# One inference step of a hybrid decoder layer in float32: two tiles of a sum trade places, and two cache copies move to another stage

## The chip, the cores and the metric

The kernel runs on one core of a Trainium2 chip. The metric is the device time of one execution in microseconds. The engines are named as in the profile: PE is the matrix engine, PEld its weight loads, DVE the vector engine, ACT the scalar engine, POOL the GpSimd engine, SP the engine that here only issues DMAs. Each engine works through its own list of instructions in order; DMAs issued by SP or ACT run on hardware queues (q1 and q10 in the profile), those issued by POOL on a software queue (q0). All of them share the sixteen DMA engines.

## What is computed

One decoder layer and a final norm for two groups of requests with the same weights: a prompt of 1024 positions and 8 samples of 8 positions, together 1088 columns. Everything is float32.

```python
def hybrid_layer(x, k_past, v_past, conv_b_past, conv_f_past, ...):
    xn = rmsnorm(x, norm1_g)
    q, k, v, glu_a, glu_b, gate_a, gate_b = jnp.split(xn @ w_in, SPLIT_IDX, axis=-1)
    ...
    branch_a = attn @ w_o_attn                    # sliding window attention, 128 wide
    u = glu_a * jax.nn.sigmoid(glu_b)
    c = dwconv_valid(jnp.concatenate([conv_b_past, u], axis=1), conv_b_w, conv_b_bias)
    branch_b = jax.nn.silu(layernorm(c, ln_b_g, ln_b_b)) @ w_pb
    merged = jax.nn.sigmoid(gate_a) * branch_a + jax.nn.sigmoid(gate_b) * branch_b
    h = x + merged @ w_out
    up = rmsnorm(h, norm2_g) @ w_up
    uc = dwconv_valid(jnp.concatenate([conv_f_past, up], axis=1), ffn_conv_w, ffn_conv_b)
    gate, val = jnp.split(uc, 2, axis=-1)
    y = h + (jax.nn.silu(gate) * val) @ w_down
```

The model width is 1024, the inner width of the feed-forward part 2816 (22 blocks of 128). Among the outputs are the new windows of the key and value caches of the samples, `concatenate([k_past, k])[:, -128:]`. Of each window 120 rows are old ones, taken over unchanged. The kernel copies them from the inputs `kpT` and `vp` to the outputs `o_kwp` and `o_vwp`, in DRAM, 960 KB each. No tile is involved.

## The kernel before

**Arithmetic.** A float32 product is made of three matmuls on rounded halves (`mm3`, L190 to L194): high times high (L192), high weight times low operand (L193), low weight times high operand (L194). Whatever goes into a matmul is therefore split first: `split_ps` (L226 to L228) makes the high half with a cast on ACT (L227) and the low half with a subtraction on DVE (L228). Weights are loaded in float32 into `wraw` (L150, L254 for the first ones) and split in the same way (L173, L174 or L227, L228).

**Stages, in the order of the program.** First the norm and the input projection, in chunks of 384, 384 and 320 columns. `norm1_load` (from L237) brings x in parts of one or two of its eight blocks of rows on SP (L242) between parts of the first three weights (L254), some of which ACT and POOL issue. `norm1_raw` splits x (L278, L279) for the first chunk, whose weights' products are scaled only afterwards; the later chunks are normed first (L347 to L349), with factors that small matmuls with an identity matrix (`identr`, cast on POOL at L847) spread over the partitions (L336). Attention, the convolution of branch B and its layer norm follow. Then comes branch A's projection (`do_o`): its result is multiplied by a gate (tile `ga`, L1010, DVE) into one of two buffers `ma`, and stored to DRAM by POOL (L1011).

`phase_z` is the projection of branch B. It computes the product of four halves with fewer multiplications, so it needs sums of the operand's quarters, T1 to T4. Each sum has two parts j, each with a high half (y = 0) and a low half (y = 1). The tiles of T1 to T3 are called `t` + x + j + y, where x counts from 0: `t111` is the low half of T2's second part, `t211` the low half of T3's second part. They are twelve tiles of 128 x 4 x 272 values in one pool, `tb`, opened when branch A's buffers are given back, and laid one behind the other in the order of `T_PLACES` (L45, L1064). A tile of the pool may be written only when whatever lay in the same bytes before is read for the last time. For the buffers `ma` that is when their store has landed.

The output projection with the second norm follows, then the feed-forward part. `ffn_up` makes the gate and value products, two blocks f = 0 and 1 plainly and the others in pairs, in the same manner with sums of quarters. Each block starts with `up_start` (L1375): a tile `st` whose first two columns are cleared on POOL (L1378), and in which the old rows of the samples are put by another POOL instruction (L1383). At f = 5 the two copies of the caches stand between these two, issued by POOL (L1381, L1382) and bound to the memset with `issue_after`. `finish` does the convolution over three positions (L1401 on ACT, L1403 on DVE), the gating and the stores (L1418 and L1424, POOL).

`ffn_down` is the last stage: two plain blocks of the down projection, `product(0)`, another plain block, `product(1)`, and the last block with the final norm. `product` calls functions from a table `hooks` at given steps (m, p) of its loop; at (0, 0) of `product(1)` two calls of `residual` (L1668) add h from DRAM to the accumulator H with an accumulating DMA on POOL.

**What sets the order.** The program only names the instructions; a planner orders each engine's list when the program is made. It takes instructions by priority, which is the place in the program plus an offset given with `self.later`, among those that are ready in its own planned time: whose inputs are made and whose buffers are free. `tc.issue_after(x)` binds an instruction behind x on its engine. On the chip each engine then keeps this order.

Of the kernel before, what the change touches and what calls it, by code (L numbers as in the profile page):

```python
# [17 lines left out]
NT = 8  # L18
# [23 lines left out]
AHEAD = 3  # L42
UP_LATER = 100
GATE_AFTER = 30
T_PLACES = ("000", "001", "200", "201", "210", "100", "211", "111", "010", "011", "101", "110")  # L45
SPLIT_AFTER = 4
GATE_LATER = 60
DOWN = ((0, 1), (2, 3), (16, 17), (18, 19, 20, 21))
# [74 lines left out]
class Build:  # L123
# [898 lines left out]
    def phase_z(self, s_es, sp, xw, sb):  # L1022
# [40 lines left out]
        at = {}  # L1063
        for tag in T_PLACES:  # L1064
            at[tag] = self.t(tb, [P, KT // 2, QW], "t" + tag, F32R)
# [267 lines left out]
    def ffn_up(self, hh, hl, mp):  # L1333
        nc, tc, a, pool = self.nc, self.tc, self.a, self.pool
# [40 lines left out]
        def up_start(f):  # L1375
            st = self.t(ft, [P, FW], "st", bufs=4)
            ss = st[:, 2 + SEQ:].rearrange("p (b t) -> p b t", b=NB)
            z = nc.gpsimd.memset(st[:, 0:2], 0.0)  # L1378
            if f == 5:
                with tc.issue_after(z.ins):  # L1380
                    nc.gpsimd.dma_start(a["o_kwp"], a["kpT"][:, :, :, NT:])  # L1381
                    nc.gpsimd.dma_start(a["o_vwp"], a["vp"][:, NT:, :])  # L1382
            nc.gpsimd.tensor_copy(ss[:, :, 0:2], co[:, f, 2:].rearrange("p (b t) -> p b t", b=NB))  # L1383

            def parts(c):
                o, n = QUARTERS[c]
                m = min(n, SEQ - o)
                yield st[:, 2 + o:2 + o + m], lambda v: v[:, :m]
                if m < n:
                    yield ss[:, :, 2:], lambda v: v[:, m:n].rearrange("p (b t) -> p b t", b=NB)  # L1390

            def ev(c, o, n, ps):
                for d, r in parts(c):
                    nc.scalar.copy(d, r(ps))
            return st, ss, parts, ev
# [40 lines left out]
        def plain(f):  # L1436
            fs = (f, NF + f)
            ws = [self.weight(("up", x), 2 - n if f == 0 else 1) for n, x in enumerate(fs)] if f == 0 else [None] * 2
            both = [up_start(x) for x in fs]
            if f == 0:  # L1440
                for c in range(4):
                    for w, b in zip(ws, both):
                        self.stream(None, xs, b[3], chunks=(c,), w=w, table=QUARTERS)
            else:
                for x, b in zip(fs, both):
                    self.stream(("up", x), xs, b[3], chunks=range(4), table=QUARTERS)
            if f == 0:
                with self.later(-60):
                    sums()
            finish(f, both, PLAIN_LATER)  # L1450
# [75 lines left out]
        def pair(f):  # L1526
            base = 7 * (f - PLAIN)
            (_, _, pg, _), (_, _, pv, _) = both = [up_start(x) for x in (f, NF + f)]
            banks = {}
            copy = nc.scalar.copy  # L1530
# [82 lines left out]
    def ffn_down(self, mp):  # L1613
        nc, a = self.nc, self.a
# [19 lines left out]
        def a_prep(n):  # L1634
            add = nc.vector.tensor_tensor
            while len(tiles) < min(n, 56):
                p = len(tiles) % 7
                a11, a21, a12, a22 = raws[len(tiles) // 7]
                r = {0: a11, 5: a12, 6: a22}.get(p)
                if r is None:  # L1640
                    sums[p] = r = self.t(aw, [P, 3, P], "as", bufs=3)
                    x, y, op = ((a21, a22, ALU.add), (a11, sums.get(1), ALU.subtract), (a12, sums.get(2), ALU.add),
                                (a21, a11, ALU.subtract))[p - 1]
                    add(r, x, y, op)
                t = self.t(aw, [P, 3, 2, P], "aw", F32R, bufs=A_AHEAD + 2)
                self.split_ps(t[:, :, 0, :], t[:, :, 1, :], r)
                tiles.append(t)
                a_load()
# [16 lines left out]
        gated = lambda f: self.g_split(f, self.g_load(f, row()), mp)  # L1665
# [7 lines left out]
        def product(s, hooks):  # L1673
            for m in range(4):
                banks = {}
                for p, (bank, fresh, row, c) in enumerate(seq):
                    n = 28 * s + 7 * m + p
                    a_prep(n + 1 + A_AHEAD)
                    w = tiles[n]
                    for j in range(2):  # L1680
                        if fresh:
                            banks[bank, j] = self.bank("mm" if bank == "A" else "aux")
                        ps = banks[bank, j][:, :QW]
                        cs = slice(j * QW, (j + 1) * QW)
                        for x in range(3):
                            b = ops[s, p, x]
                            self.mm3(ps, w[:, x, 0], w[:, x, 1], b[:, 0, cs], b[:, 1, cs], fresh and x == 0, x == 2,
                                     not fresh)
                        hs = H[:, row + m, (c + j) * QW:(c + j + 1) * QW]
                        self.added = nc.vector.tensor_tensor(hs, hs, ps, ALU.add).ins  # L1690
                    for go in hooks.get((m, p), ()):
                        go()

        def each(f, xs):
            return [lambda x=x: f(x) for x in xs]
# [25 lines left out]
        for m in range(3):  # L1721
# [2 lines left out]
        late = {divmod(2 * x, KT): [lambda i=x + 10: second(i)] for x in range(11)}  # L1724
        late[2, 2] = [lambda: a_prep(28 + A_AHEAD + 2)] + late[2, 2]
        self.down(2, H, None, late)
        product(1, {(0, 0): each(residual, (3, 7)), (2, 0): [unit], (2, 2): [unit], (2, 4): each(gated, (18,)),
                    (2, 6): each(gated, (19,)), (3, 0): each(gated, (20,)), (3, 1): [unit] + each(gated, (21,)),
                    (3, 2): [unit]})
        a_es.close()  # L1730
# [191 lines left out]
```

## Time and profile before

| | |
|---|---|
| runs | 1653.41, 1653.29, 1651.78 us; median 1653.29 |
| profiled execution | 1655.33 us, span 1653.5 us, mean granted PE clock 0.998 |
| PE, PEld | busy 1641.8 us and 1625.1 us, 11,606 matmuls |
| DVE | 1372.9 us, 2,474 instructions |
| ACT | 865.5 us, 1,795 instructions |
| POOL | 260.3 us, 551 instructions |
| DMA | 200.48 MB, 121 GB/s over the span |
| q1 (SP) | 128.52 MB, 25.0% of sixteen engines |
| q0 (POOL) | 69.75 MB, 14.2% |

The page cuts the span into forty slices of 41.3 us. This is the busy share of some of them in tenths (9 is 90% or more), and what the DMA engines did:

```profile
PE   9999999999999999999999999999999999999998
DVE  7899979999979996787755887698888787989867
POOL 0100112221011111121003421142222110000000
PEclk9999999999999999999999999999999999999999
DMA  6221222223121255647763533243333334766403
```

How to read it: PE is busy in every slice, so its gaps are too short to show here and have to be looked for in its waits and in the timeline. A timeline row is start, duration, engine, line, operation, tile written and tiles read, the shape, how many equal instructions are drawn together (x2), and in brackets the idle time of the engine just before it with the instruction that the profile takes for its releaser. A row of stretches has the stretch, its length, the busy time and count of instructions of PE, PEld, DVE, ACT and POOL, then PE's granted clock (1 is full speed), the busy share of the DMA engines and GB/s. A DMA row has the size and the time from issue to landing.

### The profile page before, as it was taken

The numbers are of one execution on the slowest core, as the hardware profiler recorded it, in microseconds if no ns is written. First come the engines' busy times: TensorE is split into PE (matmuls) and PEld (weight loads), VectorE is DVE, ScalarE is ACT, GpSimd is POOL, SyncE is SP. The second block draws the span as 40 slices with busy tenths as digits, with TensorE's granted clock in tenths as the row PEclk, the third lists the DMA queues.
The fourth block names the chain that finished last, engine by engine and source line by source line (L and its number), as shares of the span: only waits on it lengthen the run. The fifth ranks groups of instructions, "written<-read, shape, count | busy, mean of one in ns | idle before, by whom it ended". The sixth has DMA issues, their size and how long they took to land. (4 is left out here: it accounts for less than half of the span.)

```text
span 1653.5 us, 30189 instructions
## 1 busy us (share of the span) xinstructions
PE 1641.8 (99%) x11606; PEld 1625.1 (98%) x11606; DVE 1372.9 (83%) x2474; ACT 865.5 (52%) x1795; POOL 260.3 (16%) x551
## 2 busy tenths in 40 slices
PE   9999999999999999999999999999999999999998
PEld 9999999999999999999999999999999999999997
DVE  7899979999979996787755887698888787989867
ACT  6524378774488845585533454454444454524222
POOL 0100112221011111121003421142222110000000
PEclk9999999999999999999999999999999999999999
DMA  6221222223121255647763533243333334766403
GB/s 209 84 66 47 65 71 75 94 98 96 51 61 45 86 204 178 199 162 195 194 223 105 186 110 127 77 137 114 116 109 115 98 100 135 259 162 164 109 14 109
DMA packets 102497, 200.48 MB, mean 121 GB/s; under 512 B 23904, under 2 KB 54640, under 8 KB 102336
## 3 DMA queue, kind: packets, MB, share of 16 engines
q1 hardware_dynamic: 78864, 128.52, 25.0%
q0 software_dynamic: 23056, 69.75, 14.2%
q8 instruction: 91, 1.49, 0.4%
q14 instruction: 54, 0.44, 0.1%
q10 hardware_dynamic: 432, 0.27, 0.1%
HBM read 136.44 MB, written 64.03 MB: 121 GB/s over the span
## 5 line engine op out<-in xcount | busy, mean ns | idle before, releaser
L192 PE MATMUL mm<-xh,whi 128*128 128x384 f32 (+1 forms) x904 | 301.3, 333 | 0.0
L193 PE MATMUL mm<-xl,whi 128*128 128x384 f32 (+1 forms) x904 | 295.4, 327 | 0.2
L194 PE MATMUL mm<-xh,wlo 128*128 128x384 f32 (+1 forms) x904 | 295.5, 327 | 0.0
L193 PEld LDWEIGHTS mm<-xl,whi 128*128 128x128 f32 x904 | 170.0, 188 | 1.6 <-DVE xl L279 0.8
L192 PEld LDWEIGHTS mm<-xh,whi 128*128 128x128 f32 x904 | 169.9, 188 | 0.7
L194 PEld LDWEIGHTS mm<-xh,wlo 128*128 128x128 f32 x904 | 169.7, 188 | 0.1
L1403 DVE SCALAR_TENSOR_TENSOR acc<-st,fc,acc 128x1104 f32<-128x1104 f32 x88 | 119.9, 1364 | 3.7 <-ACT acc L1401 2.4
L173 ACT CAST whi<-wraw 128x1024 fp32r<-128x1024 f32 (+1 forms) x65 | 62.7, 970 | 72.9 <-PE mm L193 52.7
L227 ACT CAST whi<-wraw 128x512 fp32r<-128x512 f32 x84 | 52.6, 626 | 77.0 <-PE aux L194 36.9
L227 ACT CAST wlo<-wraw 128x512 fp32r<-128x512 f32 x84 | 52.6, 626 | 73.5 <-PE aux L194 41.3
L522 DVE SCALAR_TENSOR_TENSOR bt<-u,consts,bt 128x513 f32<-128x513 f32 x120 | 89.7, 747 | 0.7
L522 DVE SCALAR_TENSOR_TENSOR c<-sm,hsum,c 128x512 f32<-128x512 f32 x120 | 89.5, 746 | 0.7
L192 PE MATMUL mm<-mh,whi 128*128 128x272 f32 (+4 forms) x296 | 88.2, 298 | 0.0
L194 PE MATMUL mm<-mh,wlo 128*128 128x272 f32 (+4 forms) x296 | 87.9, 297 | 0.0
L228 DVE TENSOR_TENSOR wlo<-wraw,wlo 128x512 fp32r<-128x512 f32 x84 | 60.7, 723 | 29.0 <-ACT wlo L227 27.8
L522 DVE SCALAR_TENSOR_TENSOR c<-u,consts,c 128x512 f32<-128x512 f32 x112 | 83.5, 746 | 0.6
L193 PE MATMUL mm<-ml,whi 128*128 128x272 f32 (+4 forms) x280 | 82.9, 296 | 0.0
L228 DVE TENSOR_TENSOR whi<-wraw,whi 128x512 fp32r<-128x512 f32 x84 | 58.2, 694 | 28.3 <-ACT whi L227 27.2
L174 DVE TENSOR_TENSOR wlo<-wraw,whi 128x1024 fp32r<-128x1024 f32 (+1 forms) x65 | 72.6, 1121 | 8.6 <-ACT whi L173 7.2
L1555 ACT COPY st<-mm 128x272 f32<-128x272 f32 (+2 forms) x140 | 46.8, 350 | 54.4 <-PE mm L194 54.4
L192 PE MATMUL aux<-mh,whi 128*128 128x272 f32 (+4 forms) x232 | 69.7, 300 | 0.0
L193 PE MATMUL mm<-tl,wlo 128*128 128x272 f32 x240 | 69.6, 290 | 0.0
(652 smaller groups left out, 5741.3 us busy)
## 6 DMA issues: line engine op xcount, KB each, us to landing
wraw<-wall SPq DMA_DIRECT2D x118, 512.0 KB, 4.2
bw<-d_b SPq DMA_DIRECT2D x42, 272.0 KB, 4.0
d_b<-gd POOLq DMA_DIRECT2D x36, 272.0 KB, 6.1
d_b<-acc POOLq DMA_DIRECT2D x24, 272.0 KB, 3.7
ar<-wdn SPq DMA_DIRECT2D x32, 192.0 KB, 3.5
d_g<-acc POOLq DMA_DIRECT2D x10, 544.0 KB, 5.0
ga<-d_ga SPq DMA_DIRECT2D x8, 544.0 KB, 4.8
ct<-d_c SPq DMA_DIRECT2D x8, 544.0 KB, 5.6
```

Of the source, the lines that this page charges most:

```text
L173: self.cast = self.nc.scalar.copy(h[:, z], r[:, z]).ins
L174: self.nc.vector.tensor_tensor(l[:, z], r[:, z], h[:, z].bitcast(F32), ALU.subtract)
L192: mm(ps, wh, xh, start=first, stop=False, skip_group_check=more)
L193: mm(ps, wh, xl, start=False, stop=False, skip_group_check=more)
L194: self.last_mm = mm(ps, wl, xh, start=False, stop=last, skip_group_check=more).ins
L227: self.cast = self.nc.scalar.copy(h, src).ins
L228: self.low = self.nc.vector.tensor_tensor(l, src, h.bitcast(F32), ALU.subtract).ins
L522: mac = lambda o, x, w: nc.vector.scalar_tensor_tensor(o, x, w, o, ALU.mult, ALU.add)
L1403: nc.vector.scalar_tensor_tensor(acc, st[:, k:k + AW], fw(f, k), acc, ALU.mult, ALU.add)
L1555: op(d, r(ps))
```

## The change

Two edits. In `T_PLACES` the seventh and the eighth place are exchanged, so that t111 lies where t211 lay and the reverse. The two copies leave `up_start` at f = 5, and with them the binding to the memset; they become a function `windows`, called in `product(1)` at step (0, 0), behind the two residual loads. They are still issued by POOL, K before V, with the same addresses.

```diff
-T_PLACES = ("000", "001", "200", "201", "210", "100", "211", "111", "010", "011", "101", "110")
+T_PLACES = ("000", "001", "200", "201", "210", "100", "111", "211", "010", "011", "101", "110")
...
-            z = nc.gpsimd.memset(st[:, 0:2], 0.0)
-            if f == 5:
-                with tc.issue_after(z.ins):
-                    nc.gpsimd.dma_start(a["o_kwp"], a["kpT"][:, :, :, NT:])
-                    nc.gpsimd.dma_start(a["o_vwp"], a["vp"][:, NT:, :])
+            nc.gpsimd.memset(st[:, 0:2], 0.0)
             nc.gpsimd.tensor_copy(ss[:, :, 0:2], co[:, f, 2:].rearrange("p (b t) -> p b t", b=NB))
...
-        product(1, {(0, 0): each(residual, (3, 7)), (2, 0): [unit], (2, 2): [unit], (2, 4): each(gated, (18,)),
+        def windows():
+            nc.gpsimd.dma_start(a["o_kwp"], a["kpT"][:, :, :, NT:])
+            nc.gpsimd.dma_start(a["o_vwp"], a["vp"][:, NT:, :])
+
+        product(1, {(0, 0): each(residual, (3, 7)) + [windows], (2, 0): [unit], (2, 2): [unit], (2, 4): each(gated, (18,)),
```

## The prediction

> **What bounds the kernel now.** I read the page's busy times first, then the waits of the matrix engine, then stretches of the span, and the timeline only around the two places that the change touches and the one place that it may touch unasked.
>
> ```profile
> PE 1641.8 (99%) x11606; PEld 1625.1 (98%) x11606; DVE 1372.9 (83%) x2474; ACT 865.5 (52%) x1795; POOL 260.3 (16%) x551
> ```
>
> PE is busy for 1641.8 us of 1653.5, so the matmuls set the end. Nothing off PE is worth anything by itself: a gain has to be a gap on PE that closes, or a stretch at a lower clock, and a loss a new gap. The profiled execution took 1655.33 us around its span of 1653.5; the median of the runs is 1653.29, 2.04 us less. I make the sum against 1655.33 and take the 2.04 off at the end. A measurement of this kernel tells a change from none beyond about 0.2%, or 3.3 us.
>
> **The swap in T2, a gap that it can close.** On DVE and PE, where the parts of T2 are made and first used (start, duration, then the idle time before it in brackets):
>
> ```profile
> 743.26 0.71 DVE L228 TENSOR_TENSOR t<-w,t 128x544 fp32r<-128x544 f32 x1
> 746.22 1.36 DVE L228 TENSOR_TENSOR t<-w,t 128x544 fp32r<-128x544 f32 x2 [2.25 <-ACT ml L1153]
> ...
> 745.78 0.29 PE L192 MATMUL mm<-t,wlo 128*128 128x272 f32 x1
> 747.63 0.39 PE L193 MATMUL mm<-t,wlo 128*128 128x272 f32 x1 [1.56 <-DVE t L228]
> 748.23 0.39 PE L194 MATMUL mm<-t,wlo 128*128 128x272 f32 x1 [0.21 <-DVE wlo L228]
> 748.46 0.29 PE L192 MATMUL mm<-t,wlo 128*128 128x272 f32 x1
> 748.59 0.28 PE L193 MATMUL mm<-t,wlo 128*128 128x272 f32 x1
> ```
>
> The two instructions of 746.22 write tile t111, the low half of T2's second part, and PE's second matmul of 747.63 reads it. DVE stood idle for 2.25 us. The releaser named, ACT's copy at L1153, can't be it:
>
> ```profile
> 743.95 0.67 ACT L1153 COPY ml<-mm 128x272 f32<-128x272 f32 x2
> 738.22 0.56 POOL L1011 DMA_DIRECT2D d_ma<-ma  x1 [2.29 <-DVE ma L1010]
> 739.74 0.61 POOL L1011 DMA_DIRECT2D d_ma<-ma  x1
> ...
> d_ma<-ma POOLq DMA_DIRECT2D x1, 192.0 KB, 4.3
> d_ma<-ma POOLq DMA_DIRECT2D x1, 160.0 KB, 6.4
> ```
>
> That copy is done by 744.62. The last store of branch A's product was issued at 739.74 and took 6.4 us to land: 746.14, and DVE starts at 746.22. By the order of places, t111 is the eighth of twelve tiles of 4,352 bytes, and it lies over the buffer of this last store; the seventh place lies over the buffer of the store before, landed at 738.22 + 4.3 = 742.5.
>
> What it costs PE: after the matmul of 745.78 the next would start a pitch of 0.13 us later (748.46 to 748.59), at 745.91, and starts at 747.63: 1.72. The next comes 0.60 later instead of 0.13 (0.47), the one behind it 0.23 (0.10). Then PE's clock falls:
>
> ```profile
> 744.00:756.00 12.00, 10.23 (x67) 9.80 (x66) 9.63 (x18) 8.96 (x20) 0.91 (x1) 0.86 0.71 219
> 750.00:752.00 2.00, 2.00 (x10) 2.00 (x10) 2.00 (x5) 2.00 (x5) 0.00 (x0) 0.50 0.44 101
> ```
>
> In these stretches (busy time and count of PE, weight loads, DVE, ACT, POOL, then clock, DMA share, GB/s) the clock is 0.86 over twelve microseconds and 0.50 at its lowest: 0.14 × 12 = 1.7 us at most, of which I take 1.5, since the gap itself lies in the stretch. Together about 3.8.
>
> After the swap DVE need not stand at 743.97 (743.26 + 0.71), so its chain is up to 2.25 us earlier: t111 is done by 743.97 + 1.36 = 745.33, ahead of PE's 745.91. The late buffer now lies under t211, the low half of T3, which DVE writes behind this chain and so after 746.14. Next late is wlo, which DVE makes right behind t111 and PE's third matmul reads: the 0.21 of its bracket may stay. I take **−3.5 us** (bounds −3.8, and 0 if another tile is waited for at the same time).
>
> One rule of the Trainium skill would make less of it: its page "TensorE: Matmul & The Clock Gate", Part 1, has the clock fall to half after a whole activity window of about 3.4 us without work. Here a gap of 1.56 and one of 0.21 us stand before the 0.50, so by that rule alone the drop need not be the gap's, the gain would be 1.5 us smaller, and the sum 1.5 us longer.
>
> **What the copies cost in the gate stage.** At f = 5 both copies sit behind a memset, before the small copy of L1383:
>
> ```profile
> 1017.60 0.10 POOL L1378 MEMSET st<- 128x2 f32 x1 [7.20 <-DVE acc L1403]
> 1018.10 1.08 POOL L1381 DMA_DIRECT2D o_kwp<-kpT  x1 [0.40 <-issue]
> 1019.17 0.57 POOL L1382 DMA_DIRECT2D o_vwp<-vp  x1
> 1022.90 0.57 POOL L1418 DMA_DIRECT2D d_g<-acc  x1 [3.16 <-DVE acc L1416]
> 1023.48 0.21 POOL L1383 COPY st<-co 128x16 f32<-128x16 f32 x1
> ...
> q0 software_dynamic: 358, 2.00, 96.9%
> ...
> wraw<-wall SPq DMA_DIRECT2D x118, 512.0 KB, 4.2
> wraw<-wall SPq DMA_DIRECT2D x1, 512.0 KB, 8.9
> ```
>
> On the chip the issues take 1.65 us of POOL; the copies then fill 96.9% of the sixteen DMA engines for the 6.7 us from 1019.5 to 1026.2, and a weight load that starts there lands after 8.9 us instead of 4.2. PE's list of waits has no entry there. The rows show something else: L1383 stands behind a store of another step though it comes before it in the program. The order of each engine's instructions is fixed by a planner when the program is made, and it plans as if the copies held POOL far longer than they do. The next pair's order carries the mark:
>
> ```profile
> 1063.68 0.29 PE L194 MATMUL aux<-th,wlo 128*128 128x272 f32 x1
> 1064.73 0.39 PE L192 MATMUL aux<-mh,wlo 128*128 128x272 f32 x1 [0.76 <-ACT wlo L227]
> ...
> 1064.59 1.31 ACT L1401 ACTIVATE acc<-st,fc 128x1104 f32<-128x1104 f32 x1
> 1069.07 0.10 POOL L1378 MEMSET st<- 128x2 f32 x1 [16.38 <-DVE acc L1403]
> ```
>
> f = 5's convolution is put off to 1064.59 and a weight cast is late; PE's next start is 1.05 after the last instead of 0.13, with two slower ones behind it. Without the copies there the planner has no cause for it: **−1.2 us** (bounds −1.3 and 0).
>
> **Where the copies go.** The diff says: into the second product of the down projection, behind its two residual loads. But the pin is gone. In the old place `tc.issue_after(z.ins)` held them behind the memset; in the new one they stand bare, and they read inputs and write outputs, so no tile holds them back. The planner takes for each engine what is ready, and POOL is idle for 84% of the span. What it does with such instructions is seen at the start:
>
> ```profile
> 2.73 0.13 POOL L691 MEMSET u<- 128x2 f32 x1
> 12.62 0.12 POOL L690 MEMSET u<- 128x30 f32 x1 [9.75 <-DVE wlox L174]
> ```
>
> The memset of 12.62 belongs to the second convolution channel's buffer (L690, called for i = 1, far down the program), and runs as soon as DVE has let go of that buffer, which held a first weight. Copies that wait for nothing at all should come to POOL's first free moment, about 2.9 us, behind the memsets of 2.73. There the DMA engines have no room:
>
> ```profile
> q1 hardware_dynamic: 1827, 2.96, 100.4%
> ...
> 2.59 0.43 SPq L242 DMA_DIRECT2D xr<-xT  x1
> DMA to landing us min/median/max: 3.8/5.8/11.8
> 8.64 1.12 ACT L278 ACTIVATE xh<-xr,consts 128x384 fp32r<-128x384 f32 x2
> ...
> 10.21 0.34 PE L193 MATMUL mm<-xl,whi 128*128 128x384 f32 x1
> ```
>
> SP's queue alone fills them from 6 to 14 us. The copies want 0.969 × 6.7 = 6.5 us of all sixteen, so whatever is issued with or behind them lands up to 6.5 us later. The load of x issued at 2.59 brings rows 2 and 3 of eight. ACT reads them at 8.64 and needs 0.56 for one, DVE about as long for its low half, and PE's matmul of 10.21 is the first to read that: 0.4 to spare from ACT's start. The load landed between 2.59 + 3.8 = 6.4 (the shortest of x's loads) and 8.64, which is 0 to 2.2 more. Late by 6.5 it leaves PE a gap of 3.9 to 6.1; I take **+5.2**, nearer the long end because ACT's casts of weights ahead of it wait for the same DMAs. The next two loads, late by the same 6.5, then about fit behind PE's new time. If they give way to SP's queue the cost is 0; if everything waits for them with nothing to spare, 6.7. The row 8.9 against 4.2 (+4.7 while the copies alone were running) speaks for the upper end. A gap of 5 us is longer than the one above that cost 1.5 in clock: **+1.5** (0 to 1.7).
>
> The Trainium skill, page "DMA: Bandwidth & Descriptors", section "Queues, rings and completion order", says that each DMA engine goes round its queue rows and drains a whole packet of one before it turns to the next. That speaks against this place: packets of the copies would come between those of x, and the result would be near the 5.2 and not the 0; the 8.9 above agrees.
>
> Second, a planner that thinks POOL busy from 3 us on also plans POOL's next instruction, the cast of `identr` at L847, late, and with it the six small matmuls of L336 that need it:
>
> ```profile
> 27.34 0.27 PE L336 MATMUL aux<-identr,rowsl 128*128 128x128 f32 x1
> 27.45 0.39 PE L194 MATMUL aux<-xh,q 128*128 128x384 f32 x1
> 29.07 0.34 PE L194 MATMUL aux<-xh,q 128*128 128x384 f32 x1
> 29.39 0.62 PE L192 MATMUL aux<-xh,whi 128*128 128x384 f32 x2
> ```
>
> From the end of L336 (27.45) to chunk 1's first matmul (29.39) pass 1.94 us, which ACT and DVE need to scale x, covered now by ten matmuls at 0.17. If L336 is put behind those, they end at 29.24 and the 1.94 is bare: 31.18 against 29.39, **+1.8**, and some clock behind it, +0.5 (together 0 to 4).
>
> Sum: −3.5 − 1.2 + 5.2 + 1.5 + 1.8 + 0.5 = **+4.3 us**: 1655.33 + 4.3 = 1659.6 for a profiled execution, 1653.29 + 4.3 = **1657.6** for the median.
>
> **Rivals.**
>
> One, on the other side: the copies stay where the text puts them, because the planner holds them by program order. POOL's last work and its stretch:
>
> ```profile
> 1533.51 0.87 POOL L1668 DMA_DIRECT2D H<-d_h  x1 [2.64 <-DVE H L1606]
> 1530.00:1550.00 20.00, 20.00 (x159) 20.00 (x158) 17.70 (x34) 7.50 (x11) 1.74 (x2) 1.00 0.75 205
> ```
>
> They would start after 1533.51 + 0.87 = 1534.4, with PE busy for 20.00 of 20 us at a DMA share of 0.75. The copies would be covered by those matmuls, and if the cover failed they would cost at most their 6.7. Only the gains are left: 1653.29 − 4.7 = 1648.6. For it: the residual loads show POOL in program order there. Against it: those wait for H, the copies for nothing. It decides wherever the copies are issued after 1500. Chance 0.13.
>
> Two: they do come to the start but their queue gives way to SP's (the 100.4% above). Then −4.7 + 2.3: 1650.9. Against it: 8.9 beside 4.2. Chance 0.08.
>
> Three: they come to the start, and T2's wait is replaced, by another store or tile under the seventh place that comes free late. Then the 3.5 falls away: 1661.1. Against it: the store that I find there lands at 742.5, before 743.97. Chance 0.12.
>
> Four: the copies come to the front, but of a later stage (the plan may hold them at a boundary of its pools) where PE hides them; the order around them shifts by a few tenths and one or two us either way: about 1650. Chance 0.05.
>
> **How the numbers follow.** The forecast has 0.62: 1657.6, of its own from 1653.7 (a start gap of 3.9, no clock loss behind it, and half of the L336 term: 1653.29 − 4.7 + 3.9 + 1.2 = 1653.7, the least of it) to 1662. Beyond 0.2% slower means over 1656.6; within the forecast I put that at 8 in 10, in rival three at nearly all: 0.50 + 0.12 = 0.62, and 0.01 from four. Faster, under 1650.0: rival one nearly whole, half of two and of four, some 0.18. The rest, 0.19, is within. The range goes from 1650 to 1662, which leaves out most of rival one and a start that costs more than its terms.
>
> **What would show it.** The copies' row: POOL at L1724 and L1725 at about 3 us, and not at 1534. SP's loads of x with a median to landing well above 5.8 and a wait of PE for x (L278 or L279) of 4 to 6 us in the first 20; a slice of lower clock after it. L336 behind the last chunk-0 matmul. At 745 no DVE idle of 2.25 and no clock of 0.50. At f = 7 no wait of PE for the cast of L227. It would be wrong if the copies are issued in the down projection, or if they run at 3 us and PE's wait in the first 20 us stays under 2.

## The result, and the profile after

The changed kernel takes 1662.68 us in the median of six runs, the kernel before 1652.53 in six (the three shown above among them): a ratio of 1.0061 with an interval from 1.0047 to 1.0076, 10.1 us slower. Differences between runs go by this ratio, which is taken over all of them, unless medians are named; the two can differ by up to 1 us. A second comparison was made later, beside other experiments:

> The changed kernel once more, beside runs of the kernel before on the same chip. Sum of the parts as they were timed: +9.6 for the move and -2.0 for the exchange, 7.6 us (ratio 1.0046). Rival: the +10.1 of the first comparison holds (1.0061), and the exchange gains nothing beside the move.

Five runs gave 1663.36 against 1653.24, 1.0057 (1.0044 to 1.0070), 9.4 us slower: nearer the 10.1 than the 7.6 of the parts, though the interval, 7.3 to 11.6, holds both.

The profiled execution of the changed kernel took 1662.00 us with a span of 1660.2; that of before had been 1655.33 and 1653.5, so the two profiles differ by only 6.7 us. Why the runs differ by more is one of the findings below.

POOL's first instructions in the changed kernel, and PE's waits:

```profile
2.73 0.14 POOL L691 MEMSET u<- 128x2 f32 x1
2.77 1.09 POOL L1724 DMA_DIRECT2D o_kwp<-kpT  x1
3.81 0.61 POOL L1725 DMA_DIRECT2D o_vwp<-vp  x1
22.08 0.45 POOL L847 CAST identr<-consts 128x128 fp32r<-128x128 f32 x1 [17.66 <-DMA consts<-consts]
...
PE mm L192 <- ACT xh L278: 6.5, 1, 6.5
PE aux L192 <- ACT xh L348: 0.8, 1, 0.8
PE aux L317 <- ACT rstd L339: 0.6, 1, 0.6
```

Both copies went to the front of POOL's list, into the first four microseconds. PE has a wait of 6.5 us that it did not have. What is behind it, on ACT and PE, and in two stretches:

```profile
9.15 1.12 ACT L278 ACTIVATE xh<-xr,consts 128x384 fp32r<-128x384 f32 x2
12.25 0.41 ACT L173 CAST whi<-wraw 128x256 fp32r<-128x256 f32 x1 [1.97 <-DMA wraw<-wall]
17.85 0.40 ACT L173 CAST whi<-wraw 128x256 fp32r<-128x256 f32 x1 [5.20 <-DMA wraw<-wall]
19.69 1.12 ACT L278 ACTIVATE xh<-xr,consts 128x384 fp32r<-128x384 f32 x2
...
20.36 0.69 PE L192 MATMUL mm<-xh,whi 128*128 128x384 f32 x1 [6.50 <-ACT xh L278]
...
14.00:16.00 2.00, 0.00 (x0) 0.00 (x0) 0.00 (x0) 0.00 (x0) 0.00 (x0) 1.00 0.84 327
18.00:20.00 2.00, 0.00 (x0) 0.00 (x0) 1.52 (x5) 1.79 (x6) 0.00 (x0) 0.50 1.05 386
```

ACT takes its list in order. Rows 2 and 3 of x (9.15) it reads without a wait, 0.5 us later than before. At 17.85 it has waited 5.20 us for a part of a first weight, and the x blocks of 19.69, which PE wants at 20.36, stand behind that cast. PE does nothing from 14 to 20 us, and its clock is 0.50 when it goes on. The loads in question, those issued on SP between 3.6 and 6 us, first before and then after:

```profile
wraw<-wall SPq DMA_DIRECT2D x2, 256.0 KB, 5.4
xr<-xT SPq DMA_DIRECT2D x1, 384.0 KB, 5.8
```

```profile
wraw<-wall SPq DMA_DIRECT2D x2, 256.0 KB, 11.1
xr<-xT SPq DMA_DIRECT2D x1, 384.0 KB, 14.1
```

The other two places came out as the text of the change suggests. At T2, DVE and the twelve microseconds around it:

```profile
754.00 0.72 DVE L228 TENSOR_TENSOR t<-w,t 128x544 fp32r<-128x544 f32 x1
755.24 1.99 DVE L228 TENSOR_TENSOR t<-w,t 128x544 fp32r<-128x544 f32 x3
...
755.00:767.00 12.00, 12.00 (x97) 11.98 (x96) 11.85 (x22) 10.66 (x23) 0.90 (x1) 1.00 0.87 271
```

There is no idle bracket on DVE, PE is busy for 12.00 of 12 us, and the clock is 1.00. (In the second profile of this kernel, `after_again`, DVE still waits 0.33 us at this place, for a store `d_ma`; the wait of PE for `t` is gone there too.) PE's wait for a cast of L227 at f = 7, 0.8 us before, is not in the list of waits any more.

Both traces have 11,606 matmuls, so the start of the n-th can be set against the start of the n-th: how far the changed kernel is behind.

| where (time in the kernel before) | behind by, us | what happened there |
|---|---|---|
| 13.2 | 7.2 | PE's gap at the fifth row of x |
| 14.7 | 9.0 | 0.5 clock behind the gap |
| 35 | 11.7 | L336 behind chunk 0, and clock again |
| 735 | 12.0 | |
| 760 | 8.3 | T2: 3.8 back |
| 1065 to 1066 | 7.0 | f = 7: 1.3 back |
| 1452 | 6.6 | a wait of 0.3 for a bank, and what follows it, is gone |
| end | 6.7 | |

Of the first rows, 0.5 is there at 8 us already, ahead of the gap. Kernels without a copy at the start lie between 0.5 ahead (`no_copies`) and 0.4 behind (`pinned`) at that place.

### The profile page after: what moved, and what is told of

It is laid out like the page before. It is cut to its first block, busy times and chain, and to the rows that moved or that the text cites. A ratio compares the mean times of both kernels' runs of the same rounds, so it can differ in the third digit from the quotient of the medians.

```text
span 1660.2 us, 30200 instructions
## 1 busy us (share of the span) xinstructions
PE 1643.7 (99%) x11606; PEld 1627.3 (98%) x11606; DVE 1373.4 (83%) x2474; ACT 864.6 (52%) x1795; POOL 257.5 (16%) x551
## 5 line engine op out<-in xcount | busy, mean ns | idle before, releaser
L227 ACT CAST whi<-wraw 128x512 fp32r<-128x512 f32 x84 | 52.6, 626 | 75.9 <-PE aux L194 34.9
L227 ACT CAST wlo<-wraw 128x512 fp32r<-128x512 f32 x84 | 52.6, 626 | 74.7 <-PE aux L194 43.3
L193 PE MATMUL mm<-tl,whi 128*128 128x272 f32 x240 | 69.6, 290 | 0.0
```

The costliest lines, as they stand in the source:

```text
L193: mm(ps, wh, xl, start=False, stop=False, skip_group_check=more)
L227: self.cast = self.nc.scalar.copy(h, src).ins
```

## The experiments

The lag in the tables below is this one, against the profile of the kernel before, at the matmul that starts at 100 us there.

### The two edits apart

`swap_only` is the kernel before with this line exchanged, `move_only` the changed kernel with it put back:

```diff
-T_PLACES = ("000", "001", "200", "201", "210", "100", "211", "111", "010", "011", "101", "110")
+T_PLACES = ("000", "001", "200", "201", "210", "100", "111", "211", "010", "011", "101", "110")
```

> The kernel before with the two places of T2 and T3 exchanged, and nothing else. PE's lag against the kernel before, read in the two profiles matmul by matmul, falls by 3.3 us at T2. If that gap is as large in every execution (theory one), the median falls by 3.3 us (ratio 0.998). If it was large only in the execution that was profiled, which took 1655.33 us where the median of six is 1652.53 (theory two), the median falls by less than 1 us.

> The changed kernel with the old places: the copies alone are moved. Theory one (the start costs 11.7 us, the gate stage gives 1.2 back, 0.6 comes back near 1452): +9.9 us, ratio 1.006. Theory two (T2's exchange is worth nothing in most executions): the same time as the changed kernel, +10.1 us. The rival that copies at the start are covered there: within 2 us of before.

The exchange alone: 1652.20 against 1653.77, ratio 0.9988 (0.9979 to 0.9996), 2.0 us faster (1.6 in the medians). That lies between the 3.3 and the less than 1 that stood against each other, and the interval, 0.7 to 3.5, does not decide between them. The move alone: 1664.02, ratio 1.0058 (1.0044 to 1.0071), 9.6 us slower: all of the loss. In the profile of the move alone T2 still has its old place, and its wait is there, but smaller. DVE and PE there, and the stretch behind:

```profile
757.39 1.36 DVE L228 TENSOR_TENSOR t<-w,t 128x544 fp32r<-128x544 f32 x2 [1.35 <-ACT wlo L227]
758.81 0.39 PE L193 MATMUL mm<-t,wlo 128*128 128x272 f32 x1 [0.65 <-DVE t L228]
755.00:767.00 12.00, 11.15 (x86) 10.65 (x85) 10.65 (x20) 9.85 (x21) 0.90 (x1) 1.00 0.80 252
```

PE idles 0.65 us and not 1.56, and the clock stays at 1.00. So the price of T2's wait differs between executions.

### One more look at the kernel before

> The kernel before once more, for its wait at T2. If that wait is the landing of the last store and differs between executions, PE's idle at 747 is not 1.56 again (0.65 with the same places in the profile of the move alone), and the clock there may stay at 1.00. If it is fixed by the order, 1.56 and a clock of 0.50 come again.

```profile
740.23 0.60 POOL L1011 DMA_DIRECT2D d_ma<-ma  x1
d_ma<-ma POOLq DMA_DIRECT2D x1, 160.0 KB, 5.3
747.05 0.40 PE L193 MATMUL mm<-t,wlo 128*128 128x272 f32 x1 [0.52 <-DVE t L228]
744.00:756.00 12.00, 11.27 (x86) 10.76 (x86) 10.84 (x20) 10.11 (x22) 0.91 (x1) 1.00 0.79 239
```

The same program, another execution (1653.69 us): the last store lands after 5.3 us instead of 6.4, PE idles 0.52, and the clock over the twelve microseconds is 1.00 where it was 0.86. In the two traces matmul by matmul, T2 costs 2.5 us less here than in the first profile, 1.3 instead of 3.8. That is what the exchange can give back in such an execution, and the 2.0 of the runs lies between the two.

### The copies where the text of the change puts them

`pinned` is the changed kernel with the copies bound behind the last residual load; in `no_copies` the function `windows` is empty, and the two outputs are not written.

```diff
-            nc.gpsimd.dma_start(H[:, m], self.d_h[m], accum_op=ALU.add)
+            self.res = nc.gpsimd.dma_start(H[:, m], self.d_h[m], accum_op=ALU.add).ins
...
         def windows():
-            nc.gpsimd.dma_start(a["o_kwp"], a["kpT"][:, :, :, NT:])
-            nc.gpsimd.dma_start(a["o_vwp"], a["vp"][:, NT:, :])
+            with self.tc.issue_after(self.res):
+                nc.gpsimd.dma_start(a["o_kwp"], a["kpT"][:, :, :, NT:])
+                nc.gpsimd.dma_start(a["o_vwp"], a["vp"][:, NT:, :])
```

> The changed kernel with the copies bound behind the last residual load on POOL, so that they run where the text of the change has them, in the second product of the down projection. Theory one: the start is as before, and the gains are left: -3.3 - 1.2 - 0.6 = -5.1 us, ratio 0.997. Theory two: -1.8 us. Rival: the copies cost PE up to 6.7 us in the down projection too, and the time is not below that of before.

> The changed kernel without the two copies (o_kwp and o_vwp are not written). If the down projection covers the copies wholly, the same time as with the bound copies, within 0.7 us. If they cost something there, this is faster by that much.

Without copies: 1651.73, ratio 0.9982 (0.9973 to 0.9990). With the copies bound in the down projection: 1657.50, ratio 1.0021 (1.0012 to 1.0030), 3.5 us slower than the kernel before, and in the medians 5.8 slower than without copies. So the second product does not cover them. DVE, PE and the load that is late:

```profile
1549.31 0.56 DVE L1640 TENSOR_TENSOR as<-ar,ar 128x384 f32<-128x384 f32 x1 [7.14 <-DMA ar<-wdn]
1553.87 0.42 PE L192 MATMUL mm<-mh,aw 128*128 128x272 f32 x1 [3.87 <-DVE H L1686]
ar<-wdn SPq DMA_DIRECT2D x1, 192.0 KB, 13.1
```

A load of the product's weights (`ar`) lands after 13.1 us; in the profile of the kernel before the 32 loads of its kind take 3.5 in the median. DVE waits 7.14 us for it, the additions to H stand behind that in DVE's list, and PE waits 3.87 us for a bank of its accumulators that they free. It is not the residual load.

### The copies at the very end

In `tail` they leave `product(1)` and stand in `ffn_down` behind the load of `grow`, bound to a POOL instruction that reads it:

```diff
         nc.sync.dma_start(grow, a["gf"].to_broadcast([P, DM]))
+        z = nc.gpsimd.tensor_copy(self.t(dt, [P, 1], "late"), grow[:, 0:1])
+        with self.tc.issue_after(z.ins):
+            nc.gpsimd.dma_start(a["o_kwp"], a["kpT"][:, :, :, NT:])
+            nc.gpsimd.dma_start(a["o_vwp"], a["vp"][:, NT:, :])
```

> Both copies bound behind a one-column copy on POOL that reads the last vector loaded, about 1600 us, behind every residual load. If the loss with the bound copies is the wait for the last residual load, which the copies delay, nothing is lost here: the time without copies, about 2 us under the kernel before (ratio 0.998 to 0.999). If the copies cost PE something wherever they stand in the down projection, at least 2 us more than that.

```profile
1587.47 0.19 POOL L1731 COPY late<-grow 128x1 f32<-128x1 f32 x1 [58.61 <-DMA grow<-gf]
1588.36 1.08 POOL L1733 DMA_DIRECT2D o_kwp<-kpT  x1 [0.70 <-issue]
```

Issued at 1588 the copies cost nothing that can be seen: 1650.79, ratio 0.9985 (0.9976 to 0.9994), 2.5 us faster than the kernel before. The expectation named the wrong load, but the place decides as it said.

### Each copy alone at the start

In `k_floats` only the keys' copy is free and the values' is bound behind the last residual load; in `v_floats` it is the reverse. The first of them, on `pinned`:

```diff
         def windows():
+            nc.gpsimd.dma_start(a["o_kwp"], a["kpT"][:, :, :, NT:])
             with self.tc.issue_after(self.res):
-                nc.gpsimd.dma_start(a["o_kwp"], a["kpT"][:, :, :, NT:])
                 nc.gpsimd.dma_start(a["o_vwp"], a["vp"][:, NT:, :])
```

> The copy of the keys free, so that it goes to the start, that of the values bound behind the last residual load. Read is PE's lag against the kernel before from 10 to 100 us. If the delay at the start is the copies' time on the DMA engines (theory one), the keys' half makes the loads late by some 3.3 us, and PE's gap at the fourth row is 7.2 - 3.3 = about 3.9 us or less. If the values' few long packets hold the engines (theory two), the keys alone leave a gap under 2 us.

> The copy of the values free, that of the keys bound behind the last residual load. Theory one: as with the keys alone, a gap of about 3.9 us or less. Theory two: a gap of 5 us or more, nearly that of both copies. The order of the plan: if the planner takes the values' copy alone for the long occupation of POOL, the six matmuls of L336 stand behind the last matmul of chunk 0 here and not with the keys alone.

The keys alone: PE's first gap is 1.8 us (2.3 with the slower matmul behind it), no half clock, L336 in its old place, lag 2.7. The values alone, of the same 960 KB: 3.2 us (3.7), half clock, L336 behind chunk 0, lag 6.4. (Only the start is read here. In the down projection the values bound there cost PE 1.3 us in the lag, the keys bound there nothing, and both together 5.6 in `pinned`.) Neither expectation holds as it stands: the keys come out as theory two had them, the values nearer to theory one. The values' copy has two costs that the keys' has not, the plan and something on the DMA engines. Of the values alone, what ACT waits for, and two stretches while PE stands:

```profile
12.55 1.12 ACT L278 ACTIVATE xh<-xr,consts 128x384 fp32r<-128x384 f32 x2 [3.85 <-DMA xr<-xT]
...
10.00:12.00 2.00, 0.17 (x1) 0.00 (x0) 0.00 (x0) 0.00 (x0) 0.00 (x0) 1.00 0.64 224
12.00:14.00 2.00, 0.58 (x2) 0.32 (x3) 0.80 (x2) 1.45 (x4) 0.00 (x0) 1.00 0.86 307
```

Here it is rows 2 and 3 of x that come late. The DMA share is 0.64 and 0.86 while the engines wait for loads that have been issued; in the two microseconds ahead of these it is 1.11. The values' copy is one row of 122,880 bytes for each of 8 samples, and the trace has it as 16 packets of 61,440 bytes. Each of them takes about 2.3 us, never more than eight run at a time, and each of the second eight starts 0.06 us after one of the first eight has ended: eight chains of two, from 6.19 to 11.78 us, as on eight of the sixteen engines. In the changed kernel, where the keys' copy goes first, the same chains run from 11.03 to 17.12.

### The plan's part

`cast_dve` is the changed kernel with one line (L847) on another engine:

```diff
-        nc.gpsimd.tensor_copy(self.identr, self.ident)
+        nc.vector.tensor_copy(self.identr, self.ident)
```

> The changed kernel with the cast of identr on DVE in place of POOL, so that PE's order at the start is that of the kernel before again while both copies stay at 2.77 us. If the late place of L336 is a cost of its own (the prediction's +2.3), PE's lag at 100 us falls from 11.7 to 9.4 and the median is 2.3 us under that of the changed kernel. Rival: x's first normed block is late by the loads anyway, and the lag stays above 11.

PE's order at the start is that of before again, the copies stay where they are, the first gap is 6.9 (6.7 in the changed kernel): the lag falls from 11.7 to 8.9. Runs: 1661.21, ratio 1.0046 (1.0030 to 1.0063), 1.5 to 2.2 under the two medians of the changed kernel. The late L336 is a cost of its own. Its size differs between executions: 2.6 in the first profile of the changed kernel, where half clock follows it, and 1.1 in `after_again` and `move_only`, where none does. What goes before it differs too: the lag at 20 us is 9.0 in the first and 10.7 and 10.0 in the others.

### The long packets' part

The same copy in rows of 4,096 bytes, in an order that doesn't join them:

```diff
-            nc.gpsimd.dma_start(a["o_vwp"], a["vp"][:, NT:, :])
+            nc.gpsimd.dma_start(a["o_vwp"].rearrange("b (x y) c -> x b (y c)", y=4),
+                                a["vp"][:, NT:, :].rearrange("b (x y) c -> x b (y c)", y=4))
```

`v_cut` does this to `v_floats`, `both_cut` to the changed kernel.

> As the values' copy alone at the start, but written in rows of 4,096 bytes in an order that doesn't join them. If the long packets held some DMA engines while others stood idle, PE's first gap falls from 3.7 us to that of the keys' copy, 1.9 to 2.6, with no stretch at half clock. If only the bytes count, 3.7 us again.

> The changed kernel with the values' copy in rows of 4,096 bytes. Theory of the long packets: PE's first gap falls from 7.2 to about 5 us, the lag at 100 us to about 7, and the median to some 4 us above that of before. Theory of the bytes: gap 7.2, lag 9.4 as with the cast on DVE, +7.9 us.

In both, L336 went back to its old place without any other edit: what makes the planner hold POOL's next instruction is the form of the values' copy. The stretch of `v_cut` that answers to the first of the two above, and the first gap of `both_cut`:

```profile
10.00:12.00 2.00, 0.90 (x4) 0.64 (x4) 1.13 (x3) 1.53 (x3) 0.00 (x0) 1.00 1.02 396
```

```profile
18.57 0.45 PE L192 MATMUL mm<-xh,whi 128*128 128x384 f32 x1 [4.79 <-ACT xh L278]
```

The values alone now cost a lag of 2.2 instead of 6.4. Read at 20 us, ahead of L336, it is 2.2 instead of 5.3; the plan has no part in that. Both together: lag 7.4 (8.9 with the cast on DVE, which has the long packets and the old order), PE's wait 4.8; runs 1658.70, ratio 1.0034 (1.0020 to 1.0047), 5.6 us over before. So, by these profiles, the lag of 11.7 is 7.4 for the copies' bytes, 1.5 for the long packets and 2.7 for the plan. The last two are rough, since three profiles of the same start differ by 1.6 at 20 us; the runs have 2.0 for the long packets (7.6 against 5.6), with intervals that overlap. Clear of that is only the fall from 5.3 to 2.2 with the values alone.

### Other places early in the program

`behind_cast` is the changed kernel with the copies bound behind the cast of `identr`. `mid` has `self.first_store`, the first gate store (L743), in its place, and `mid_cut` is `mid` with the values' copy cut.

```diff
         def windows():
-            nc.gpsimd.dma_start(a["o_kwp"], a["kpT"][:, :, :, NT:])
-            nc.gpsimd.dma_start(a["o_vwp"], a["vp"][:, NT:, :])
+            with self.tc.issue_after(self.ident_cast):
+                nc.gpsimd.dma_start(a["o_kwp"], a["kpT"][:, :, :, NT:])
+                nc.gpsimd.dma_start(a["o_vwp"], a["vp"][:, NT:, :])
```

> The copies bound behind the cast of identr on POOL, some 14 us, while the DMA engines are still full until 26 us. If it is the first chunk's loads that count, PE's gap at the fourth row is gone, and the lag at 100 us is what the later loads cost. The second chunk's loads are then late by 6.5 us against a slack of about 2: a lag of 4 to 8 us. Rival: these loads have slack enough, and the lag is under 1.

> The copies bound behind the first gate store (L743), about 43 us, where the DMA engines are idle (share 0.00 from 30 to 40 us). If a place costs what its DMA traffic is late by, the start costs nothing here and the time is that of the bound copies at the end, about 1650.8 (ratio 0.9985). Rival: the planner's long occupation of POOL shifts the stores behind it, and PE loses 1 us or more.

> The copies bound behind the first gate store, with the values' copy in rows of 4,096 bytes. If the +19 us there were the planner's occupation of POOL, which goes with the form of that copy, nothing is lost and the time is that of the bound copies at the end (1650.8, ratio 0.9985). If it was the DMA traffic, +10 us or more remain.

`behind_cast`: issued at 14.38 and 15.43, the copies cost nothing until 64 us, so the second chunk's loads had slack enough, against my first expectation; but then a wait of 2.6 us with clock behind it, lag 4.3: POOL stands for 23.13 us in front of a store (L719) that comes ahead of gate stores here. `mid` is the worst of all: 1672.62, ratio 1.0114 (1.0099 to 1.0130), lag 21. PE's waits and POOL's list there:

```profile
PE mm L192 <- DVE q L764: 8.5, 1, 8.5
PE mm L192 <- ACT gt L224: 8.5, 1, 8.5
...
46.51 1.12 POOL L743 DMA_DIRECT2D d_ga<-gt  x2 [0.71 <-DVE gt L742]
67.36 0.54 POOL L719 DMA_DIRECT2D o_cbp<-u  x1 [19.73 <-DVE u L936]
77.15 0.54 POOL L743 DMA_DIRECT2D d_gb<-gt  x1 [7.41 <-ACT gt L224]
```

In `mid` too POOL stands in front of this store, for 19.73 us, because DVE has its data only at 67, and the gate stores come behind it. That the planner put it ahead of them because it took POOL for occupied by the copies is inferred from the orders. `mid_cut` moves the same bytes at the same place: 1651.39, ratio 0.9989 (0.9980 to 0.9999), lag -0.1. POOL's list there has that store behind the gate stores, as in the kernel before. The 21 us were the plan, and the DMA traffic at 43 us costs nothing (in `mid` too the lag is 0.4 up to 64 us).

### The copies in their old place, cut

`f5_cut` is `swap_only` with the values' copy cut in the same way.

> The kernel before with the places exchanged and the values' copy in rows of 4,096 bytes, the copies still at f = 5. If the stall of the pair at f = 7 came from the planned occupation, it is gone (1.0 to 1.2 us in the lag) and the time is that of the copies at the end, about 1650.8. If it came from the DMA traffic or the issues, it stays.

`f5_cut` takes 1650.88, ratio 0.9985 (0.9976 to 0.9995), 2.5 us faster than before. PE's wait at f = 7, 0.8 us in the list of `swap_only` as in that of before, is gone and the lag falls by 1.3 there, with the copies still issued at f = 5 (1015.48 us in its trace) and long landed when PE comes to f = 7. So that stall was the planned occupation too. With `tail` this is the best version run that keeps the copies. The runs do not tell these two apart, nor either of them from `mid_cut` (0.9989) or `swap_only` (0.9988).

## Why the prediction was right or wrong

It forecast slower by 4.3 us, 1657.6 and at most 1662.0; the runs gave 1662.68, slower by 10.1. The sign and the mechanism hold, the size doesn't. Point by point:

**The copies leave the down projection.** Right, and the whole loss hangs on it: POOL issues them at 2.77 and 3.81, where the prediction had 2.9.

**The start, +5.2 and +1.5.** The step that failed. Its reasoning took the first load hurt to be that of x's rows 2 and 3, late by the 6.5 us that the copies need on the DMA engines. Those rows were still in time. Late were the loads behind them, which it had let "about fit" behind PE's new time: the last parts of the first weights, which ACT casts ahead of the next rows, and these rows themselves, which landed 8.3 us later (14.1 against 5.8). PE was 0.5 behind ahead of its gap, the gap at the fifth row took 6.7, and the slower clock behind it 1.8: 9.0 instead of 6.7 (10.7 and 10.0 in two other profiles of this start). The load that the prediction named is the one that comes late where the values' copy is issued first (`v_floats`, 3.85 us of wait on ACT). Of the difference, some 1.5 is what the values' long packets add (`cast_dve` against `both_cut`): the 6.5 counted bytes only. They run in eight chains of two, and while they hold what must be eight engines the DMA share falls to 0.64 with loads outstanding. That a load then waits for its part on those eight is inferred, since the trace does not name the engine of a packet. On this the Trainium skill ("DMA: Bandwidth & Descriptors", "Queues, rings and completion order") has each DMA engine drain a whole packet before it turns to another queue. The fall of the lag at 20 us from 5.3 to 2.2 in `v_cut` fits that.

**L336, +1.8 and +0.5.** Right in mechanism and about in size: 2.6 in the lag of the first profile, 1.1 where no half clock follows, 1.5 to 2.2 in the runs. The cause is narrower than it was put: not POOL's two issues but the form of the values' copy alone.

**T2, -3.5.** Right for the execution from which it was worked out (3.8 back in the profiles), and mis-sized for the median: 2.0 in the runs (0.7 to 3.5). The rows were those of an execution with a late store and half a clock behind it; in two others the wait cost 1.3 to 1.4. The profiled execution's 2.04 us over the median were a sign of it, and the prediction took them off at the end as if they had nothing to do with the term. The rule of the Trainium skill that was weighed there ("TensorE: Matmul & The Clock Gate", Part 1, half clock after a whole window without work) does not account for the 0.50 behind 1.56 us; the 1.00 behind 0.65 and 0.52 us does not contradict it. The sum with a gain of 2.0 at T2, as the runs have it, would have been 1.5 longer and nearer.

**The gate stage, -1.2.** Right in size (1.3 in the lag) and cause (`f5_cut`). One sign of it was misread: the store that stands ahead of L1383 at f = 5 stands there in `f5_cut` too, where the stall is gone.

**Rival one, the copies stay in the down projection: 1648.6.** Wrong in its price too. `pinned` is that case, and takes 3.5 us more than before: PE was busy for 20.00 of 20 us there, but its weights' loads had no slack for the copies. Of the others, two (their queue gives way) and four (a later stage) fall with the 6.5 us of PE's wait and the issue at 2.77, and three with the missing bracket at T2; only in `after_again` does DVE wait there for a store, 0.33 us, and PE does not.

Put together with the runs' sizes: 11.7 - 2.0 - 1.3 - 0.6 = 7.8. The runs say 10.1 and, the second time, 9.4, with intervals from 7.3 to 12.6, so the sum lies at their lower edge. The second profiles of the two kernels come nearer. `after_again` (1663.36) against `before_look` (1653.69), matmul by matmul, is 9.7 us: 11.5 at 100 us, 0.7 back at T2, 0.6 lost again at 770, 1.3 back at f = 7, 0.3 at 1620, and the rest small. The 6.7 of the first two profiles was small because that execution of the kernel before, at 1655.33 against a median of 1652.53, paid the long wait at T2. How much the exchange gives in a usual execution stays open: 0.7 to 3.8 in the profiles.

## What to carry to other kernels

A transfer that depends on nothing has no place in a program unless it is bound to one: a planner that takes what is ready will issue it first, and there it meets the loads that the first matmuls wait for. A stretch in which PE is fully busy covers a transfer only if the loads of that stretch have slack; look for the next load on each queue, not for the busy share. And a wait that ends with a DMA's landing should be priced from more than one execution.

## What the runs showed of the hardware that was not expected

Of two copies of 960 KB, each alone at the start, the one in packets of 4,320 bytes put PE 2.7 us behind at 20 us, the one in sixteen packets of 61,440 bytes 5.3; cut into rows of 4,096 bytes the second put it 2.2 behind. A gap of 1.56 us on PE was followed by a clock of 0.50 in one execution, gaps of 0.65 and 0.52 us at the same place by 1.00 in two others. But a gap of 1.67 us at the start of `k_floats` was followed by 1.00 as well, so the length of the gap alone does not decide it.
